# Both halves of k's remainder over 128 rows, and weight remainders computed ahead into DRAM, in a two-block network on one core

## The chip, the cores and the metric

One core of a Trainium2 chip runs the whole kernel. The metric is the device time of one execution in microseconds. The engines that matter here are TensorE (PE in the profile, with its weight loads as PEld), VectorE (DVE), ScalarE (ACT), and SyncE (SP), whose queue issues the DMAs.

## The reference, cut

Two blocks follow each other on a sequence of 512 positions of width 1024. The first has two layers, each a mixer (mLSTM, HGRN2 and sliding-window attention side by side), an MLP and a gated per-layer embedding. The second has two layers, each an attention (dilated in layer 0, differential in layer 1), a cross attention to 256 memory positions and a SwiGLU network. All is float32.

```python
for l in range(DEPTH):                                   # first block
    y = _rms_norm(x, in_norm_g[l]) @ w_in[l] + b_in[l]
    ...
    x = x + jnp.concatenate([m_out, h_out, s_out], axis=-1) @ w_out[l]
    u = _rms_norm(x, mlp_norm_g[l]) @ w_up[l]
    x = x + jnp.square(jax.nn.relu(u)) @ w_down[l]
    ...
# second block, differential attention (layer 1); layer 0 takes the same scores with dilated masks
sc = jnp.einsum('bhcqd,bhckd->bhcqk', qblk, k, preferred_element_type=f32) * scale
p = jax.nn.softmax(sc, axis=-1)
a = p[:, :, 0] - lam * p[:, :, 1]
return jnp.einsum('bhqk,bhkd->bhqd', a.astype(v.dtype), v, preferred_element_type=f32)
```

Heads are 64 wide, so two heads share 128 partitions.

## The kernel before

**Number format.** A float32 operand is held as two fp32r tiles: a rounded high part (made by a ScalarE cast) and the remainder, called the lower half (made by a VectorE subtraction). A product is three matmuls, hi·hi, lo·hi and hi·lo (`mm3`). For the scores of 64-wide heads there are stacks instead: `q_stacks` puts the high part of q in the head's own 64 rows of one tile `qs` and the lower half in the other 64; `k_stacks` puts the high part of k into both halves of `kh`. One 128-row matmul of `qs` and `kh` then gives q_hi·k_hi + q_lo·k_hi. The lower half `kl` is only in the head's own 64 rows, and a second matmul over these 64 rows adds q_hi·k_lo. That is so in the attentions (`score`, lines 1735 to 1742) and in the mLSTM (lines 1381 to 1383). The sliding-window heads ask for `both=True` and fill `kl` in both halves by a second VectorE subtraction.

**Stages.** One program runs the stages b10, mlp0, ple0, b11, mlp1, ple1, attn0, cross0, ffn0, attn1, cross1, ffn1 in this order; b10 and b11 are the mixers of the first block, the last digit is the layer. In mlp a block of 8 GEMMs with `w_up` and 8 with `w_down` is repeated four times; a GEMM is one weight tile of 128x1024 and 24 matmuls of 512 columns. In attn each of 8 pairs of heads makes q and k by two GEMMs, rotates them, builds the stacks, computes the scores, the softmax and the product with v, while GEMMs of the pairs after it stand between. In cross the memory's K and V are made from `xk` and `xv` in pieces of 512 columns (`mem_kv`), as a filling between other work.

**Weights.** `Weights.load` calls `wload` (line 789): SP loads the raw weight into `wr`, ScalarE casts it to `wh`, VectorE subtracts to `wl`. Tile counts are fixed by line 673, `NT, NWH, NWR, NKR, NKH = 58, 5, 3, 2, 2`: five of `wh` and of `wl`, three raw ones; the small pieces of `xk` and `xv` have two raw tiles `kr` and two each of `kh` and `kl` of their own. In a mixer 34 + 12 + 32 loads over the two layers carry its weights; all of them need the subtraction.

**What sets the order.** Code is not issued as written. A `Recorder` notes every operation; a list scheduler (`schedule`) with planned costs, dependences and tile counts puts them in order on each engine, and `emit` writes that order out. So every instruction has the line of the one `getattr` call in `emit` (L670 before, L674 after), and the profile is read by the tiles' names: `wr`, `wh`, `wl` for weights, `kr`, `kh`, `kl` for small pieces and for k, `g` and `s` for PSUM banks, `hi`, `lo` for activations. A DMA stands in SP's order and waits there until its tile is free; nothing behind it is issued meanwhile.

## Time and profile before

| | |
|---|---|
| median of 3 runs | 3096.06 us (3095.2 to 3097.9) |
| profiled execution | 3094.59 us, its span 3092.8 us |
| granted TensorE clock, mean | 0.981 |
| TensorE busy | 3024.8 us (98%), 16672 matmuls |
| weight loads of TensorE busy | 2463.1 us (80%) |
| VectorE busy | 1922.2 us (62%), 3811 instructions |
| ScalarE busy | 1490.9 us (48%), 2731 instructions |
| DMA | 269.96 MB, mean 87 GB/s |

Busy shares are means over stages that differ much, so the trace is read by stage. The stages end at about 300, 632, 690, 1000, 1330, 1390, 1660, 1855, 2250, 2515, 2697 and 3093 us of the span; neighbours overlap by some us. Matmuls are pipelined: a row's duration is longer than the distance to the next start, and it is the distance that tells what a matmul costs.

### The profile page before, as it was taken

To read this page: it belongs to the slowest core of one execution; us is meant where nothing else is said; L and a number is where in the kernel's file an instruction comes from. 1 tells how busy PE (TensorE), PEld (TensorE's weight loads), DVE (VectorE), ACT (ScalarE), POOL (GpSimd) and SP (SyncE) were. 2 spreads that over 40 slices of the span, in tenths; PEclk is the share of its full clock that TensorE was granted. 3 is DMA by queue.
4 is the path that set the end of the run, shared out by engine and by line. 5 is a ranking of instruction groups with operands and counts; after the bars stand their busy time and mean duration, and the time that the engine had idled before them with its cause. 6 is when DMAs were issued, how large, how long until landed. Compare 5 with 4: busy or idle time off the path is not lost.

```text
span 3092.8 us, 42875 instructions
## 1 busy us (share of the span) xinstructions
PE 3024.8 (98%) x16672; PEld 2463.1 (80%) x16672; DVE 1922.2 (62%) x3811; ACT 1490.9 (48%) x2731; POOL 75.0 (2%) x91
## 2 busy tenths in 40 slices
PE   8999999999999999999999999999999999999998
PEld 6767888887767888887776888888887778988887
DVE  7868444478878544467657756333489867653435
ACT  7557333346567333345667544222366665542223
POOL 0010000000010000000000000000000000000000
PEclk9989999999989999999999999999999999999999
DMA  3302222321312323222111423222322223332223
GB/s 119 96 12 80 102 95 96 99 91 59 106 46 63 112 96 99 98 94 77 42 55 63 125 74 102 100 97 96 102 87 71 66 65 103 97 116 96 96 98 100
DMA packets 86611, 269.96 MB, mean 87 GB/s; under 512 B 9608, under 2 KB 12680, under 8 KB 86408
## 3 DMA queue, kind: packets, MB, share of 16 engines
q1 hardware_dynamic: 86408, 267.22, 26.7%
q8 instruction: 131, 2.15, 0.3%
q14 instruction: 72, 0.59, 0.1%
HBM read 265.09 MB, written 2.10 MB: 86 GB/s over the span
## 4 chain that ended last, share of the span: by engine, by line
PE 90%; DVE 6%; ACT 2%; DMA 1%; issue 1%; POOL 0%; POOLq 0%; DVEq 0%; ACTq 0%; SPq 0%
PE s L670 47%; PE g L670 39%; PE t L670 4%; DVE wl L670 1%; DVE y L670 1%; DVE G L670 0%; ACT kh L670 0%; DVE X L670 0%; ACT wh L670 0%; DMA kr<-in_xk_dram 0%; DVE kl L670 0%; DVE B L670 0%; DMA wr<-in_w_in_tm_dram 0%; DVE x L670 0%; ACT L670 0%
## 5 line engine op out<-in xcount | busy, mean ns | idle before, releaser
L670 ACT CAST wh<-wr 128x1024 fp32r<-128x1024 f32 (+2 forms) x482 | 483.5, 1006 | 1086.0 <-PE s L670 394.3
L670 DVE TENSOR_TENSOR wl<-wr,wh 128x1024 fp32r<-128x1024 f32 (+2 forms) x482 | 560.3, 1164 | 233.8 <-ACT wh L670 226.0
L670 PE MATMUL g<-hi,wh 128*128 128x512 f32 (+1 forms) x1756 | 679.0, 387 | 12.3 <-ACT hi L670 9.3
L670 PE MATMUL g<-hi,wl 128*128 128x512 f32 (+1 forms) x1756 | 678.0, 386 | 1.5 <-DVE wl L670 1.5
L670 PE MATMUL g<-lo,wh 128*128 128x512 f32 (+1 forms) x1756 | 678.6, 387 | 0.1
L670 PE MATMUL s<-hi,wh 128*128 128x512 f32 (+1 forms) x1732 | 652.2, 377 | 2.5 <-ACT hi L670 2.4
L670 PE MATMUL s<-lo,wh 128*128 128x512 f32 (+1 forms) x1732 | 651.5, 377 | 2.0 <-DVE lo L670 2.0
L670 PE MATMUL s<-hi,wl 128*128 128x512 f32 (+1 forms) x1732 | 652.2, 377 | 0.0
L670 PEld LDWEIGHTS g<-hi,wh 128*128 128x128 f32 x1756 | 333.5, 190 | 78.9 <-ACT hi L670 10.9
L670 PEld LDWEIGHTS g<-hi,wl 128*128 128x128 f32 x1756 | 333.9, 190 | 65.4 <-issue 6.4
L670 PEld LDWEIGHTS g<-lo,wh 128*128 128x128 f32 x1756 | 333.5, 190 | 63.4 <-issue 4.9
L670 PEld LDWEIGHTS s<-hi,wh 128*128 128x128 f32 x1732 | 326.1, 188 | 62.1 <-ACT hi L670 4.1
L670 PEld LDWEIGHTS s<-lo,wh 128*128 128x128 f32 x1732 | 326.2, 188 | 60.6 <-DVE lo L670 3.1
L670 PEld LDWEIGHTS s<-hi,wl 128*128 128x128 f32 x1732 | 326.2, 188 | 57.6 <-issue 1.2
L670 ACT ACTIVATE P<-P,s 128x512 f32<-128x512 f32 (+1 forms) x224 | 137.6, 627 | 25.0 <-DVE s L670 24.4
L670 POOL TENSOR_TENSOR s<-s,mhalf 128x4 f32<-128x4 f32 (+2 forms) x53 | 69.0, 1303 | 2864.9 <-DVE s L670 2423.9
L670 ACT ACTIVATE hi<-x,cols 128x512 fp32r<-128x512 f32 (+1 forms) x112 | 73.5, 659 | 68.5 <-DVE x L670 67.8
L670 PE MATMUL t<-const,P 128*128 128x128 f32 x560 | 96.8, 281 | 1.5 <-ACT P L670 1.0
L670 PE MATMUL g<-wh,hi 128*128 128x256 f32 (+1 forms) x304 | 91.2, 301 | 0.1
L670 PE MATMUL g<-wh,lo 128*128 128x256 f32 (+1 forms) x304 | 91.1, 300 | 0.0
L670 PE MATMUL g<-wl,hi 128*128 128x256 f32 (+1 forms) x304 | 90.9, 299 | 0.0
L670 DVE TENSOR_TENSOR u<-s,R 128x512 f32<-128x512 f32 x39 | 27.0, 692 | 101.0 <-PE s L670 101.0
(300 smaller groups left out, 4058.2 us busy)
## 6 DMA issues: line engine op xcount, KB each, us to landing
wr<-in_w_down_dram SPq DMA_DIRECT2D x96, 512.0 KB, 3.3
wr<-in_gu_dram SPq DMA_DIRECT2D x88, 512.0 KB, 3.3
wr<-in_w_up_dram SPq DMA_DIRECT2D x64, 512.0 KB, 3.3
wr<-in_w_in_fm_dram SPq DMA_DIRECT2D x34, 512.0 KB, 3.3
wr<-in_qk_dram SPq DMA_DIRECT2D x32, 512.0 KB, 3.3
wr<-in_xo_dram SPq DMA_DIRECT2D x24, 512.0 KB, 3.5
wr<-in_w_down_dram SPq DMA_DIRECT2D x32, 384.0 KB, 3.2
wr<-in_w_out_dram SPq DMA_DIRECT2D x32, 256.0 KB, 2.7
```

Source lines behind the costliest of these rows:

```text
L670: getattr(getattr(nc, o.eng), o.fn)(*[res(a) for a in o.args], **{k: res(v) for k, v in o.kw.items()})
```

## The change

Three things are altered. First, `k_stacks` fills `kl` in both halves for all its callers, by a ScalarE copy of the own half; the second matmul of a score then runs over 128 rows, in the attentions and in the mLSTM, and adds q_lo·k_lo as well. Second, `lows` makes the lower halves of later weights in pieces of 512 columns (a load into `kr`, a cast to `kh`, a subtraction to `kl`, a store to a DRAM tile `dl`), 206 pieces in all: 62 in mlp0 (for the weights of b11), 64 in mlp1 (`xk`, `xv`, `ao`, `xq` of layer 0) and 80 in ffn0 (`qk`, `v`, `xk`, `xv` of layer 1). `work` puts them behind the evacuations of the GEMMs, one to three at a time. Third, `wload` of such a weight loads `wl` (or `kl`) from that DRAM tile in SP's queue in place of the subtraction. The rest (`psum`, `after`) keeps the recorder right with the new DRAM pool.

```diff
+        self.psum = space is not None and space is not DRAM
...
+        if self.after is not None:
+            deps.add(self.after)
...
-        return self.b.wload(src, n, self.small), k1 - k0, c1 - c0
+        lows = self.b.pre.get(id(self.ap))
+        return self.b.wload(src, n, self.small, lows and lows[self.i - 1]), k1 - k0, c1 - c0
...
+        self.dp = nc.pool("dp", 1, DRAM)
+        self.pre, self.jobs = {}, []
...
-    def wload(self, src, n, small=False):
+    def wload(self, src, n, small=False, low=None):
         nc = self.nc
         if small:
             raw = self.kr.tile([P, T], F32, name=self.nm("kr"), tag="kr")[:, :n]
...
             lo = self.wp.tile([P, 1024], F32R, name=self.nm("wl"), tag="wl")[:, :n]
         nc.sync.dma_start(raw, src)
         nc.scalar.copy(hi, raw)
-        nc.vector.tensor_tensor(lo, raw, hi.bitcast(F32), op=ALU.subtract)
+        if low is None:
+            nc.vector.tensor_tensor(lo, raw, hi.bitcast(F32), op=ALU.subtract)
+        else:
+            nc.sync.dma_start(lo.bitcast(F32), low)
         return hi, lo
+
+    def lows(self, name, plan):
+
+        nc, ap = self.nc, self.a[name]
+        out = self.pre[id(ap)] = []
+        o = 0
+        for k0, k1, c0, c1 in plan:
+            n = (k1 - k0) * (c1 - c0)
+            out.append(self.dp.tile([P, n], F32, name=self.nm("dl"), tag=f"{name}_{len(out)}"))
+            for s in range(0, n, T):
+                m = min(T, n - s)
+                raw = self.kr.tile([P, T], F32, name=self.nm("kr"), tag="kr")[:, :m]
+                hi = self.kp.tile([P, T], F32R, name=self.nm("kh"), tag="kh")[:, :m]
+                lo = self.kp.tile([P, T], F32R, name=self.nm("kl"), tag="kl")[:, :m]
+                nc.after = nc.ops[-1]
+                nc.sync.dma_start(raw, bass.AP(tensor=ap.tensor, offset=ap.offset + o + s, ap=[[n, P], [1, m]]))
+                nc.after = None
+                nc.scalar.copy(hi, raw)
+                nc.vector.tensor_tensor(lo, raw, hi.bitcast(F32), op=ALU.subtract)
+                nc.sync.dma_start(out[-1][:, s:s + m], lo.bitcast(F32))
+                yield
+            o += n * P
+
+    def ahead(self, *names):
+
+        for name, plan in names:
+            self.jobs.append(self.lows(name, PLANS[plan]))
+
+    def work(self, n=1):
+        while n and self.jobs:
+            try:
+                next(self.jobs[0])
+                n -= 1
+            except StopIteration:
+                self.jobs.pop(0)
+
+    def work_all(self):
+        while self.jobs:
+            self.work()
...
-    def k_stacks(self, k, both=False):
-
+    def k_stacks(self, k):
         nc = self.nc
         out = []
         for h in range(2):
...
             nc.scalar.copy(hi[own], k[own])
             nc.scalar.copy(hi[oth], k[own])
             nc.vector.tensor_tensor(lo[own], k[own], hi[own].bitcast(F32), op=ALU.subtract)
-            if both:
-                nc.vector.tensor_tensor(lo[oth], k[own], hi[own].bitcast(F32), op=ALU.subtract)
+            nc.scalar.copy(lo[oth], lo[own].bitcast(F32))
             out.append((hi, lo))
...
                 nc.tensor.matmul(sb, kh[:, s], qs[hh][:, t0:], start=True, stop=False)
-                own = slice(64 * hh, 64 * hh + 64)
-                nc.tensor.matmul(sb, kl[own, s], qs[hh][own, t0:], start=False, stop=True)
+                nc.tensor.matmul(sb, kl[:, s], qs[hh][:, t0:], start=False, stop=True)
                 nc.vector.tensor_tensor(W[j], sb[:, j * P - t0:], W[j], op=ALU.mult)
                 As[hh, j] = W[j]
         o = self.obank()
...
         wd = Weights(self, self.a[f"w_down{l}"], PLANS["w_down"])
         st2 = self.stats()
+        if l == 0:
+            self.ahead(("w_in_fm1", "w_in_fm"), ("w_in_tm1", "w_in_tm"), ("w_out1", "w_out"))
+        else:
+            self.ahead(("xk0", "xk"), ("xv0", "xv"), ("ao0", "sq"), ("xq0", "sq"))
         for c in range(4):
             hid = []
 
...
                 nc.vector.tensor_scalar(u, o, 0.0, None, op0=ALU.max)
                 nc.scalar.activation(u, u, AF.Square)
                 hid.append(self.split(u))
+                self.work()
 
             self.gemm(wu, ops, 8, evac)
 
...
                 nc.vector.tensor_tensor(self.x[j], self.x[j], u, op=ALU.add)
                 if c == 3:
                     self.updated(st2, j)
+                else:
+                    self.work(1 + j % 2)
 
             self.gemm(wd, hid, KT, evac2)
+        self.work_all()
         return st2
 
     def ple(self, l, st):
...
-    def score(self, h, q, k, c, mask):
+    def score(self, q, k, c, mask):
         nc = self.nc
         s = self.sbank()
         kh, kl = k
         nc.tensor.matmul(s, q[:, c * P:c * P + P], kh, start=True, stop=False)
-        own = slice(64 * h, 64 * h + 64)
-        nc.tensor.matmul(s, q[own, c * P:c * P + P], kl[own], start=False, stop=True)
+        nc.tensor.matmul(s, q[:, c * P:c * P + P], kl, start=False, stop=True)
         p = self.f("P")
         mx, dn = self.small(1), self.small(1)
         if mask is None:
...
         ys = [None] * KT
+        if l == 0:
+            self.ahead(("qk1", "qk"), ("v1", "v"), ("xk1", "xk"), ("xv1", "xv"))
         for c, nh in enumerate((8, 8, 6)):
             hid = []
             for j in range(nh):
...
                 nc.scalar.activation(t, t, AF.Silu, bias=0.0)
                 nc.vector.tensor_tensor(t, u, t, op=ALU.mult)
                 hid.append(self.split(t))
+                self.work(3)
 
             def evac(j, o):
                 if c == 0:
...
 
             if c < 2:
                 self.gemm(wd, hid, KT, evac)
+        self.work_all()
         st2 = {"halves": [], "ops": []}
         mark = wd.i, wd.o
         for u, h in enumerate(HALVES):
```

What the change does to the order on the engines is shown at three places, each before and after, word for word.

SP's queue in mlp1, at the turn from `w_up` to `w_down`; each row is one DMA, the tile it writes and what it reads. Before:

```order
L670 DMA wr_9911<-in_w_up_dram 128x1024
L670 DMA wr_9945<-in_w_up_dram 128x1024
L670 DMA wr_9979<-in_w_up_dram 128x1024
L670 DMA wr_10013<-in_w_up_dram 128x1024
L670 DMA wr_10049<-in_w_down_dram 128x1024
L670 DMA wr_10087<-in_w_down_dram 128x1024
L670 DMA wr_10125<-in_w_down_dram 128x1024
```

After:

```order
L674 DMA dl_11297<-kl_11290 128x512
L674 DMA kr_11303<-in_xv_dram 128x512
L674 DMA wr_11328<-in_w_down_dram 128x1024
L674 DMA dl_11342<-kl_11336 128x512
L674 DMA kr_11364<-in_xv_dram 128x512
L674 DMA wr_11374<-in_w_down_dram 128x1024
L674 DMA dl_11400<-kl_11390 128x512
L674 DMA kr_11407<-in_xv_dram 128x512
L674 DMA wr_11420<-in_w_down_dram 128x1024
L674 DMA dl_11439<-kl_11434 128x512
```

Between two weight loads there now stand a store of one piece's lower half and the load of a later piece.

VectorE in attn1, about the middle of the stage, between the rotation and the stacks of one pair of heads and the transposed probabilities (`Tl`) of another. Before:

```order
L670 TENSOR_TENSOR qs_21807<-z_21669,qs_21807 64x512
L670 TENSOR_TENSOR wl_21876<-wr_21448,wh_21638 128x1024
L670 TENSOR_TENSOR Tl_21849<-t_21860,Th_21834 128x2x128
L670 TENSOR_TENSOR Tl_21854<-t_21860,Th_21839 128x2x128
L670 TENSOR_TENSOR kl_21903<-z_21773,kh_21870 64x512
L670 TENSOR_TENSOR kl_21910<-z_21773,kh_21890 64x512
L670 SCALAR_TENSOR_TENSOR vl_21917<-s_21736,s_20045,vh_21816 128x256
L670 SCALAR_TENSOR_TENSOR vl_21917<-g_21795,s_20045,vh_21816 128x256
```

After:

```order
L674 SCALAR_TENSOR_TENSOR vl_23223<-g_23096,s_21317,vh_23121 128x256
L674 TENSOR_SCALAR s_23244<-s_23244 128x1
L674 TENSOR_TENSOR kl_23261<-kr_23212,kh_23249 128x512
L674 RECIPROCAL s_23257<-s_23257 128x1
L674 TENSOR_TENSOR kl_23276<-z_23089,kh_23216 64x512
L674 TENSOR_TENSOR Tl_23237<-t_23247,Th_23228 128x2x128
L674 TENSOR_TENSOR Tl_23241<-t_23247,Th_23233 128x2x128
```

The subtraction for a weight of this stage (`wl`) is gone; in its place stands one for a piece (`kl` from `kr`, 128x512) that ffn0's part of the program had begun to list.

TensorE in cross0, in the products that make the memory's K (`kh`, `kl` are a piece of `xk`, `hi` and `lo` the memory's activations, 128x256). Before, at the seam of two pieces:

```order
L670 MATMUL g_15245<-hi_8198,kh_15285 128x256
L670 MATMUL g_15245<-hi_8198,kl_15294 128x256
L670 MATMUL g_15245<-lo_9027,kh_15285 128x256
L670 MATMUL g_15245<-hi_8114,kh_15292 128x256
L670 MATMUL g_15245<-hi_8114,kl_15301 128x256
L670 MATMUL g_15245<-lo_8122,kh_15292 128x256
L670 MATMUL g_15245<-hi_8114,kh_15292 128x256
```

After, at the seam of two pieces:

```order
L674 MATMUL g_16265<-hi_8617,kl_16328 128x256
L674 MATMUL g_16265<-lo_8629,kh_16331 128x256
L674 MATMUL s_16387<-hi_8471,kh_16365 128x256
L674 MATMUL g_16326<-lo_16359,wh_16034 128x512
L674 MATMUL g_16392<-hi_16300,wh_16061 128x512
L674 MATMUL g_16392<-hi_16300,wl_16045 128x512
L674 MATMUL g_16326<-hi_16384,wh_16034 128x512
L674 MATMUL s_16387<-hi_8471,kl_16362 128x256
L674 MATMUL s_16387<-lo_8485,kh_16365 128x256
L674 MATMUL s_16387<-hi_8471,kh_16365 128x256
```

GEMM matmuls of 512 columns now stand between the pieces, which followed each other directly.

## Rows read from the trace of the kernel before

**Rows 1.** The chain that ended last, its shares by engine.

```profile
PE 90%; DVE 6%; ACT 2%; DMA 1%; issue 1%; POOL 0%; POOLq 0%; DVEq 0%; ACTq 0%; SPq 0%
```

**Rows 2.** Windows of eight stages: b10, mlp0, b11, attn0, cross0, ffn0, attn1, cross1.

```profile
core 0: us, PE busy (x) PEld busy (x) DVE busy (x) ACT busy (x) POOL busy (x), PEclk, DMA share, GB/s
0.00:300.00 300.00, 273.04 (x1839) 206.09 (x1840) 230.05 (x630) 192.12 (x445) 21.95 (x44) 0.91 0.24 74
300.00:632.00 332.00, 332.00 (x1481) 274.81 (x1480) 164.27 (x199) 111.62 (x142) 1.01 (x1) 1.00 0.30 100
690.00:1000.00 310.00, 290.82 (x1844) 221.37 (x1843) 253.86 (x661) 203.34 (x463) 16.92 (x14) 0.92 0.22 66
1390.00:1660.00 270.00, 269.98 (x1467) 198.06 (x1466) 184.99 (x444) 173.00 (x322) 1.01 (x1) 1.00 0.19 63
1660.00:1855.00 195.00, 192.08 (x1188) 161.92 (x1189) 124.68 (x264) 109.00 (x210) 3.51 (x3) 0.99 0.28 87
1855.00:2250.00 395.00, 394.31 (x1937) 331.26 (x1936) 174.58 (x222) 129.49 (x180) 4.29 (x4) 1.00 0.31 100
2250.00:2515.00 265.00, 262.92 (x1609) 210.15 (x1608) 236.87 (x586) 177.00 (x373) 11.50 (x10) 1.00 0.20 65
2515.00:2697.00 182.00, 177.27 (x1216) 159.16 (x1215) 118.91 (x230) 94.47 (x183) 4.25 (x4) 0.99 0.32 101
```

**Rows 3.** Timeline of TensorE in attn0: start, duration (us), operation, shapes.

```profile
1509.60 0.39 PE L670 MATMUL g<-lo,wh 128*128 128x512 f32 x1
1509.83 0.40 PE L670 MATMUL g<-hi,wh 128*128 128x512 f32 x1
...
1510.52 0.40 PE L670 MATMUL s<-kh,qs 128*128 128x512 f32 x1
1510.85 0.50 PE L670 MATMUL s<-kl,qs 64*128 64x512 f32 x1
1511.28 0.50 PE L670 MATMUL g<-hi,wh 128*128 128x512 f32 x1
1511.62 0.40 PE L670 MATMUL s<-kh,qs 128*128 128x512 f32 x1
```

**Rows 4.** Timeline of TensorE in b10's sliding-window heads.

```profile
260.62 0.28 PE L670 MATMUL s<-kh,qs 128*128 128x256 f32 x1
260.74 0.28 PE L670 MATMUL s<-kl,qs 128*128 128x256 f32 x1
```

**Rows 5.** Tile kl, its score matmuls: count, ns min/median/max, starts, forms.

```profile
L670 PE MATMUL s<-kl,qs x192: 277/492/562, 233.2 to 2511.4; 64*128 64x512 f32 x128, 128*128 128x256 f32 x64
L670 PE MATMUL s<-qs,kl x32: 335/579/792, 157.7 to 894.5; 64*128 64x256 f32 x16, 64*128 64x512 f32 x8, 64*128 64x384 f32 x8
```

**Rows 6.** Groups by form: shapes, count, busy us, mean ns, idle before.

```profile
L670 DVE TENSOR_TENSOR wl<-wr,wh 128x1024 fp32r<-128x1024 f32 x406 | 495.3, 1222 | 219.4 <-ACT wh L670 212.3 <-PE s L670 6.2
L670 ACT CAST kh<-z 64x512 fp32r<-64x512 f32 x72 | 44.5, 618 | 24.3 <-DVE z L670 23.0
L670 DVE TENSOR_TENSOR kl<-kr,kh 128x512 fp32r<-128x512 f32 x64 | 43.4, 687 | 16.3 <-ACT kh L670 15.1 <-PE s L670 0.9
L670 ACT CAST kh<-kr 128x512 fp32r<-128x512 f32 x64 | 39.1, 617 | 27.6 <-DMA kr<-in_xv_dram 10.8 <-DMA kr<-in_xk_dram 10.0 <-PE g L670 2.7
```

**Rows 7.** Timeline of TensorE in b11's mLSTM.

```profile
893.49 0.58 PE L670 MATMUL s<-qs,kl 64*128 64x256 f32 x1
893.99 0.58 PE L670 MATMUL s<-qs,kh 128*128 128x256 f32 x1
```

**Rows 8.** Window of b11, VectorE's instructions on tile wl alone.

```profile
690.00:1000.00 310.00, 37.87 (x40) 0.92 0.22 66
```

**Rows 9.** Loads of xk's pieces, from issue to landing.

```profile
DMA to landing us min/median/max: 2.5/3.1/5.2
```

**Rows 10.** DMA issues of xq: count, KB each, median us to landing.

```profile
wr<-in_xq_dram SPq DMA_DIRECT2D x16, 512.0 KB, 3.9
```

**Rows 11.** Waits of SP's queue: total us, times, longest.

```profile
SPq L670 <- DVE wl L670: 2381.5, 436, 51.7
```

More of the change, by code (lines that the diff above doesn't have):

```diff
@@ L17 @@
 PSUM = bass.MemoryType.PSUM
+DRAM = bass.MemoryType.DRAM
 P = 128
@@ L307, in __init__ @@
         self.ops, self.pools = [], []
-        self.single = None
+        self.single = self.after = None
         for e in ("tensor", "vector", "scalar", "gpsimd", "sync", "either"):
@@ L333, in add @@
             for wb, w in v.tile.writes:
-                if v.tile.pool.space is not None and w.eng == "tensor" or \
+                if v.tile.pool.psum and w.eng == "tensor" or \
                         wb[0] <= b[1] and b[0] <= wb[1] and wb[2] <= b[3] and b[2] <= wb[3]:
@@ L341, in add @@
                     if (wb[0] <= b[1] and b[0] <= wb[1] and wb[2] <= b[3] and b[2] <= wb[3]) or \
-                            (v.tile.pool.space is not None and eng == "tensor"):
+                            (v.tile.pool.psum and eng == "tensor"):
                         deps.add(w)
@@ L364, in add @@
                 t.left += 1
-        o.banks = [t for t in o.tiles if t.pool.space is not None] if eng != "tensor" else []
+        o.banks = [t for t in o.tiles if t.pool.psum] if eng != "tensor" else []
+        if self.after is not None:
+            deps.add(self.after)
         o.deps = [d for d in deps if d is not o]
@@ L398, in locks @@
             return False
-        psum = lambda v: v.tile.pool.space is not None
+        psum = lambda v: v.tile.pool.psum
         ptr = o.fn in ("tensor_scalar", "scalar_tensor_tensor")
@@ L410, in cost @@
         n = int(np.prod(o.args[0].shape[1:])) if isinstance(o.args[0], View) else 512
-        psum = any(v.tile.pool.space is not None for v in ins + outs)
+        psum = any(v.tile.pool.psum for v in ins + outs)
         if o.eng == "tensor":
@@ L429, in cost @@
             acc = 93.0 if "accum_out" in o.kw else 0.0
-            return (51.0 if (ins or outs)[0].tile.pool.space is not None else 93.0) + n * ACT_EL + PTR_A * ptr + acc, 130.0
+            return (51.0 if (ins or outs)[0].tile.pool.psum else 93.0) + n * ACT_EL + PTR_A * ptr + acc, 130.0
         if o.eng == "vector":
@@ L1098, in block1 @@
         sw = self.swa_prep(l, lambda: fm_id(F_SK), "swk")
-        ks = self.k_stacks(sw, True)
+        ks = self.k_stacks(sw)
         m0 = self.mlstm(l, 0, mq[0], mk[0], tm, rows)
@@ L1661, in attn @@
                 for c2 in range(2):
-                    pr = [[self.score(h, qs[h], ks[h], 2 * c2 + c, dil[2 * c2 + c]) for h in range(2)] for c in range(2)]
+                    pr = [[self.score(qs[h], ks[h], 2 * c2 + c, dil[2 * c2 + c]) for h in range(2)] for c in range(2)]
                     for c in range(2):
@@ L1694, in attn @@
                         c = 2 * c2 + cc
-                        p0, d0 = self.score(0, qs[0], ks[0], c, None)
-                        p1, d1 = self.score(1, qs[1], ks[1], c, None)
+                        p0, d0 = self.score(qs[0], ks[0], c, None)
+                        p1, d1 = self.score(qs[1], ks[1], c, None)
                         nc.vector.reciprocal(d0, d0)
```

## The prediction

> **What bounds the kernel now.** I read the chain of waits first: TensorE carries 90% of the chain that ended last [rows 1]. Then the table by stage [rows 2]: in two of the large GEMM stages, mlp0 and ffn0, TensorE is busy 332.0 of 332.0 us and 394.3 of 395.0; in the two attention stages 270.0 of 270.0 and 262.9 of 265.0. VectorE is far behind everywhere but in attn1 (236.9 of 265.0) and in the mixer block b11 (253.9 of 310.0, where TensorE idles 19.2 us). So what counts is TensorE's own time, and VectorE's load only in b11 and attn1.
>
> A busy TensorE isn't one at its peak, so I then read starts in the timeline. In attn0 a 128x512 GEMM matmul follows the one before it after 0.23 us (1509.60 to 1509.83). Around the product with k's lower half, which has 64 rows (64*128), it does not: from kh at 1510.52 to the next kh at 1511.62, three matmuls of 512 columns take 1.10 us, where 3 x 0.23 = 0.69 would do: 0.41 us more for one 64-row matmul, spread over its neighbours [rows 3]. The control is in the same kernel: the sliding-window heads already hold both halves of k, their lower product has 128 rows, and the next matmul starts 0.12 us behind, as it should with 256 columns [rows 4]. There are 128 such matmuls of 64 rows in the attention stages (192 less the 64 of the sliding window) and 32 in the mLSTM [rows 5].
>
> A rule speaks against this reading. The Trainium skill (TensorE: Matmul & The Clock Gate, What overlaps and what doesn't) says that a weight load overlaps with running matmuls only if its row group differs, and another table of that page that a single product with few rows takes the same time as one with 128; by the two nothing would be won, and D below is that case. The trace disagrees with the first: 128-row products one behind the other keep 0.23 and 0.12 us. The Trainium skill (TensorEngine Tiling (Array Packing), Key Properties) also says that a change of tiling mode drains the engine; the trace agrees, if 64 rows are such a mode: 0.41 us for going there and back.
>
> **The change part by part.**
>
> *k over 128 rows in attention.* Columns stay, so TensorE loses only the 0.41 us: 64 x 0.41 = 26 us in attn0 and as much in attn1. Added: one ScalarE copy for each half head, 16 x 0.618 = 9.9 us per stage [rows 6], which stands between VectorE's subtraction and the lower product. In attn0 TensorE then needs 270 - 26 = 244 us; ScalarE 173 + 10 = 183 and VectorE's 185 stay under it. TensorE has GEMMs of the next heads to fill in. I take 24 of 26; the floor is 10, should the copy hold up each of the 16 chains by about a microsecond.
>
> *attn1.* Its 24 weights of qk and v lose their subtraction, 24 x 1.222 = 29.3 us of VectorE [rows 6]. But the change's order shows that not all jobs fit in ffn0: behind ffn0's last weight load 35 of its 80 stores are still to come, and subtractions of theirs stand in attn1's VectorE order between those of the heads. At most that gives back 35 x 0.687 = 24.0 us, and on ScalarE 35 x 0.617 = 21.6 beside 9.9 for copies. So VectorE goes from 236.9 to about 232, ScalarE from 177 to 208, TensorE from 265 to 239. VectorE rises from 89% to 97% of the stage's length: it is nearly a second bound, and a cast that waits for its load stands in ScalarE's queue ahead of the heads' exponentials. I take 15 of 26; ends 3 and 26.
>
> *mLSTM.* 16 matmuls of 64 rows in each of b10 and b11. They start 0.50 us apart with 256 columns, against 0.12 [rows 4, 7]; part of that is the lower clock there (granted 0.91 and 0.92 on average). Price each between 0.41 us and 2 x 0.38 = 0.76: 6.6 to 12.2 us per layer. TensorE idles 27.0 and 19.2 us in these stages for other engines, so some of it turns into waiting: I take 4 in each, ends 0 and 12.
>
> *Weights of b11.* 40 subtractions leave VectorE, 37.9 us of 253.9 [rows 2, 8]. That can free no more than TensorE's idle 19.2 us. Few of the 40 lie where TensorE idles, so I take 5 us; ends 0 and 19.
>
> *Lower halves loaded, cross0 and cross1.* The 64 pieces of xk and xv use two small buffers. Before, a free one was refilled by a cast and a subtraction (0.617 + 0.687 us); now the lower half comes by a load, 3.1 us after its issue in the median, 2.5 at best [rows 9], and it can't be issued until TensorE has read the buffer. A piece is 12 matmuls x 0.12 = 1.44 us; the order lets 3 to 5 GEMM matmuls (0.23 each, some 0.9) stand between pieces, so a refill has 1.44 + 2 x 0.9 = 3.2 us. Load and need are even; 0.1 us lost at each piece makes 64 x 0.1 = 6 us. Lower end: 7.6 us won (TensorE's idle time there, 2.9 and 4.7 us). Upper end: 64 x 0.7 = 45 lost, if these loads rise to the 3.9 us of xq's [rows 10]. I stay near even, since 3.1 is the row of these very pieces. VectorE's relief (32 x 0.687 = 22 us in cross1) buys little: it is busy 118.9 of 182 there.
>
> *The jobs in mlp0, mlp1 and ffn0.* 206 pieces: load, cast 0.617, subtraction 0.687, store, 256 KB each way. VectorE goes from 164 to 164 + 62 x 0.687 = 207 of 332 us in mlp0, ScalarE to 150. No wait ends late there; the data rate rises from 100 GB/s by 62 x 0.52 MB / 332 us = 97, the DMA share from 0.30 to about 0.6. What hides this is the lead of the weight loads: SP waits 2381.5 us in total for VectorE's subtractions to free a raw buffer, so loads are nearly always early [rows 11]. One new wait sits in SP's queue: the order there is weight, store, small load, and the store waits for the cast and subtraction of the load before it, with the next weight load behind it. One turn costs 3.1 + 0.62 + 0.69 = 4.4 us and the hand-overs between engines, and TensorE eats a weight in 24 x 0.23 = 5.5. It fits, by 1.1 us for the hand-overs. I take 0; its other end is the slower rival below.
>
> Sum: -24 -15 -4 -4 -5 +6 = -46. The profiled execution took 3094.6 us (span 3092.8), so 3048.6; the median of the runs lies 1.5 above it, so 3050.
>
> **The rivals.**
> (B) attn1 becomes VectorE's and the pieces wait for their loads: attn1 gives 5 instead of 15, the crosses cost 20 instead of 6: 3050 + 24 = 3074. For it: 97% in attn1, the two buffers. Against it: VectorE at 89% of attn1 now leaves TensorE only 2.1 us idle.
> (C) The relief is worth nearly all it can be: 25 + 23 in attention, 19 + 4 in b11, 4 in b10, and the crosses win 4: 3096 - 79 = 3017. Against it: the leftover jobs in attn1.
> (D) The 0.41 us doesn't come from the rows but from the change of operands, which stays. Then only b11's 5 us are won and the crosses' 6 lost: 3097, within 0.2%. Against it: [rows 4], where the operands change as often.
> (E) Slower: SP's queue paces TensorE in mlp0 and mlp1, where there is about one job for one weight (62 + 52 turns). It decides from a turn of 5.5 us. If the small loads land after 5.2 us, the longest of xk's [rows 9], since two more streams share the DMA engines, a turn is 6.5: 114 x 1.0 = 114 us, less a lead of three weights in each stage (2 x 16.5), so 81 on 3050: 3131. For it: the doubled DMA share. Against it: 5.2 is one row's end, the median 3.1, and many of these loads ran beside weight loads too.
>
> **How the numbers follow.** Forecast as summed, 3050: 0.66. B 0.14, C 0.10, D 0.04, E 0.06. What a measurement of this kernel can tell from no change is about 0.2%, here 6 us: 3090 to 3102. Faster: the forecast, B and C, 0.90; same: D, 0.04; slower: E, 0.06. The forecast's own ends come from attn1 (3 to 26), attn0 (10 to 26), b11 and the crosses: some 3030 to 3070. The range reaches to B and close to C: 3020 to 3080.
>
> **What would show it.** In the profile after, the groups of 64 rows are gone, the product with kl starts 0.23 us behind kh's, and attn0 is near 246 us. attn1 near 250 with VectorE over 90%: right; over 260: B. mlp0, mlp1 and ffn0 keep their lengths within 2 us, else E, and TensorE then waits for the cast or the subtraction of a weight. In cross0 and cross1 I look for TensorE waiting for loads of kl. I'm wrong at the root if the pitch around kl stays 0.4 us at 128 rows.

## The result, and the profile after

The changed kernel takes 3045.36 us in the median of 4 runs (3044.07 to 3050.5), against 3096.66 before: ratio 0.984, 95% interval 0.982 to 0.986. 51 us went; 46 were forecast. The unchanged kernel was run beside each batch of kernels below; its median there lies between 3094.97 and 3097.4.

The table by stage of the kernel after (columns as in [rows 2]; b10, mlp0, b11, attn0, cross0, ffn0, attn1, cross1). In every kernel below a stage ends where TensorE starts the GEMM matmul with the same number, counting those that read a weight, as at the stage's end in the kernel before.

```profile
core 0: us, PE busy (x) PEld busy (x) DVE busy (x) ACT busy (x) POOL busy (x), PEclk, DMA share, GB/s
0.00:296.90 296.90, 267.61 (x1839) 206.41 (x1840) 228.52 (x628) 194.76 (x451) 21.94 (x44) 0.92 0.23 75
296.90:628.90 332.00, 332.00 (x1481) 274.80 (x1480) 200.08 (x259) 148.59 (x203) 1.01 (x1) 1.00 0.60 195
686.90:967.10 280.20, 271.30 (x1839) 211.11 (x1838) 220.24 (x623) 202.41 (x467) 19.76 (x14) 0.98 0.40 128
1356.90:1610.80 253.90, 252.62 (x1475) 199.35 (x1474) 185.04 (x457) 183.51 (x345) 1.01 (x1) 1.00 0.25 84
1610.80:1802.90 192.10, 187.20 (x1184) 159.38 (x1183) 90.05 (x209) 106.67 (x208) 2.71 (x3) 1.00 0.48 157
1802.90:2201.20 398.30, 392.30 (x1888) 326.97 (x1888) 194.12 (x255) 152.89 (x215) 4.32 (x4) 0.99 0.47 157
2201.20:2462.10 260.90, 250.38 (x1628) 213.65 (x1627) 233.09 (x601) 206.21 (x429) 9.46 (x10) 1.00 0.56 186
2462.10:2646.20 184.10, 180.58 (x1245) 161.33 (x1244) 107.34 (x208) 98.22 (x188) 3.72 (x4) 1.00 0.47 150
```

Against [rows 2]: mlp0 is 332.0 us as before, with the DMA share at 0.60 instead of 0.30 and TensorE never idle. b11 fell from 310 to 280 us: TensorE's idle time from 19.2 to 8.9, and its mean granted clock rose from 0.92 to 0.98. attn0 fell from 270 to 254, attn1 only from 265 to 261, with TensorE's idle time up from 2.1 to 10.5 us; ffn0 grew by 3.

The products with k's lower half, in attn0 after (start, duration, operation):

```profile
1474.78 0.40 PE L674 MATMUL s<-kh,qs 128*128 128x512 f32 x1
1475.02 0.39 PE L674 MATMUL s<-kl,qs 128*128 128x512 f32 x1
1475.24 0.40 PE L674 MATMUL g<-hi,wh 128*128 128x512 f32 x1
```

kl starts 0.24 us behind kh and the GEMM 0.22 us behind kl; in [rows 3] these were 0.33 and 0.43.

Stage lengths against the kernel before, in us, of all kernels run (each from its profiled execution; mlp0 and ple0 stay within 0.1, and mlp1, ple1 and ffn1 within 1.0 but for ple1 in pieces64, +2.9; attn and cross are taken together, since work moves over their border). One execution scatters: in b10 the order of TensorE's matmuls is the same in after, k_only and all kernels from b11_qkv1 to b11, and their b10 lies anywhere from -1.3 to -4.4. So a difference below some 3 us between two rows of this table is not told apart from none.

| kernel | median, us | ratio, interval | b10 | b11 | attn0 + cross0 | ffn0 | attn1 + cross1 |
|---|---|---|---|---|---|---|---|
| after | 3045.36 | 0.984 (0.982 to 0.986) | -3.2 | -29.8 | -18.9 | +3.3 | -2.0 |
| k_only | 3042.79 | 0.983 (0.981 to 0.984) | -2.5 | -11.9 | -20.2 | 0.0 | -16.3 |
| lows_only | 3100.66 | 1.0015 (1.0005 to 1.0026) | +3.5 | -23.8 | +1.8 | +2.0 | +20.6 |
| k_attn | 3053.83 | 0.987 (0.985 to 0.989) | -3.7 | +3.0 | -22.4 | 0.0 | -17.4 |
| b11_qkv1 | 3026.3 | 0.977 (0.976 to 0.978) | -3.3 | -29.5 | -19.3 | +2.6 | -18.5 |
| m0m1_qkv1 | 3025.47 | 0.977 (0.976 to 0.979) | -2.2 | -29.3 | -18.3 | +1.5 | -18.3 |
| pieces64 | 3043.22 | 0.983 (0.982 to 0.985) | -2.8 | -30.2 | -20.3 | +2.9 | -4.9 |
| dma_only | 3038.07 | 0.981 (0.980 to 0.983) | -2.7 | -30.2 | -18.5 | +2.6 | -7.8 |
| early32 | 3026.66 | 0.978 (0.976 to 0.979) | -1.3 | -30.3 | -20.7 | +1.6 | -17.5 |
| b11 | 3026.1 | 0.977 (0.976 to 0.979) | -4.4 | -28.0 | -17.9 | +0.2 | -17.2 |
| swa64 | 3125.88 | 1.0095 (1.008 to 1.011) | +18.6 | +12.2 | +0.5 | -0.1 | +1.5 |

### The profile page after: what moved, and what is told of

Its sections match the earlier page's. It is cut to its first block, busy times and chain, and to the rows that moved or that the text cites. A ratio compares the mean times of both kernels' runs of the same rounds, so it can differ in the third digit from the quotient of the medians.

```text
span 3042.3 us, 44343 instructions
## 1 busy us (share of the span) xinstructions
PE 2966.3 (98%) x16672; PEld 2453.6 (81%) x16672; DVE 1923.8 (63%) x3870; ACT 1627.0 (53%) x2975; POOL 73.3 (2%) x91
## 4 chain that ended last, share of the span: by engine, by line
PE 84%; ACT 6%; DVE 6%; DMA 3%; issue 1%; POOL 0%; SPq 0%; POOLq 0%; ACTq 0%; DVEq 0%
PE s L674 42%; PE g L674 38%; PE t L674 4%; ACT kh L674 1%; ACT P L674 1%; DMA kl<-dl 1%; ACT wh L674 1%; DVE wl L674 1%; DVE sh L674 1%; DVE s L674 1%; DVE y L674 0%; DVE z L674 0%; DVE cv L674 0%; ACT kl L674 0%; DMA kr<-in_xq_dram 0%
## 5 line engine op out<-in xcount | busy, mean ns | idle before, releaser
L674 DVE TENSOR_TENSOR wl<-wr,wh 128x1024 fp32r<-128x1024 f32 (+2 forms) x403 | 474.7, 1179 | 405.3 <-PE s L674 131.8
L674 ACT CAST kh<-kr 128x512 fp32r<-128x512 f32 (+2 forms) x270 | 166.0, 616 | 125.9 <-DMA kr<-in_xk_dram 24.9
L674 DVE TENSOR_TENSOR kl<-kr,kh 128x512 fp32r<-128x512 f32 (+2 forms) x206 | 141.1, 685 | 66.8 <-ACT kh L674 65.1
L674 DVE SCALAR_TENSOR_TENSOR lo<-x,cols,hi 128x512 fp32r<-128x512 f32 (+1 forms) x112 | 74.7, 672 | 24.7 <-ACT hi L674 24.2
```

Source lines behind the costliest of these rows:

```text
L674: getattr(getattr(nc, o.eng), o.fn)(*[res(a) for a in o.args], **{k: res(v) for k, v in o.kw.items()})
```

## The experiments

### The two parts apart: k_only and lows_only

k_only keeps the change of `k_stacks`, `score` and the mLSTM and lists no work ahead:

```diff
         if l == 0:
-            self.ahead(("w_in_fm1", "w_in_fm"), ("w_in_tm1", "w_in_tm"), ("w_out1", "w_out"))
+            pass
         else:
-            self.ahead(("xk0", "xk"), ("xv0", "xv"), ("ao0", "sq"), ("xq0", "sq"))
+            pass
...
-            self.ahead(("qk1", "qk"), ("v1", "v"), ("xk1", "xk"), ("xv1", "xv"))
+            pass
```

> Only k over 128 rows; no lower half is made ahead, every weight keeps its subtraction. Theory 1 (two separate gains: k's rows give the attention stages and b10 theirs, the weights' relief gives b11 most of its 30 us): b10 -3, attn0 with cross0 -19, attn1 -14 since no leftover pieces stand in it, b11 -5 to -10, the others within 1: 3096 - 44 = 3052, between 3048 and 3060. Theory 2 (b11's 30 us come from k's rows in the mLSTM, which end its stretches at half the clock): b11 -25 here, so 3096 - 61 = 3035. Theory 3 (attn1 is bound by VectorE, with or without leftovers): attn1 -4 as in the changed kernel.

lows_only puts the three functions back as they were and keeps everything else:

```diff
-            nc.scalar.copy(lo[oth], lo[own].bitcast(F32))
+            if both:
+                nc.vector.tensor_tensor(lo[oth], k[own], hi[own].bitcast(F32), op=ALU.subtract)
...
-        nc.tensor.matmul(s, q[:, c * P:c * P + P], kl, start=False, stop=True)
+        own = slice(64 * h, 64 * h + 64)
+        nc.tensor.matmul(s, q[own, c * P:c * P + P], kl[own], start=False, stop=True)
```

> Only the lower halves made ahead and loaded; k's remainder stays over 64 rows in attention and mLSTM, as before the change. Theory 1: b11 -20 to -25, attn0 0, attn1 +3 to +8 (leftover pieces, no shorter products), ffn0 +3, cross within 3: 3096 - 15 = 3081, between 3074 and 3088. Theory 2: b11 -5, and the rest as in theory 1: 3098. Theory 1 also asks that the half-speed stretches of b11 go from 47.7 us to about 15 or less here; theory 2 that they stay above 35.

k's rows alone make the whole gain: 3042.79 us, which can't be told from the full change (the intervals overlap). The work ahead alone is 0.15% slower than before. So k's rows make the size of the full change's 51 us; the work ahead wins in b11 and loses as much in other places. Windows of k_only (b11, attn0, attn1; columns as above):

```profile
687.60:985.60 298.00, 278.79 (x1838) 217.77 (x1838) 252.70 (x661) 205.29 (x471) 17.23 (x14) 0.94 0.22 71
1375.40:1626.50 251.10, 250.65 (x1459) 198.49 (x1459) 180.70 (x442) 175.98 (x331) 1.01 (x1) 1.00 0.21 68
2215.10:2466.30 251.20, 244.87 (x1609) 211.29 (x1608) 236.10 (x592) 186.24 (x392) 11.65 (x10) 1.00 0.22 70
```

and of lows_only (b11, attn1):

```profile
693.60:979.70 286.10, 277.58 (x1839) 212.92 (x1837) 221.85 (x625) 198.74 (x461) 19.90 (x14) 0.97 0.39 125
2233.30:2514.20 280.90, 274.23 (x1625) 215.31 (x1624) 234.89 (x601) 197.65 (x414) 9.91 (x10) 0.98 0.51 170
```

In b11 VectorE is busy 252.7 us with k's rows alone and 221.9 with the work ahead alone; the stage shrinks by 11.9 and 23.8 us, by 29.8 with both. So theory 2 falls: b11 gets the larger part from the weights' relief, 29.8 - 11.9 = 18 us beside k's rows, and with the work ahead alone its mean clock is 0.97. The time that b11 spends at half the clock, on which the expectation also turned, goes from 47.7 us to 17 in lows_only and to 34 in k_only. In attn1 lows_only has 281 us where the kernel before had 265. Theory 1 holds in its split, but both its times were missed. Its 3052 for k_only was 9 us too much, outside the 3048 to 3060 that I had put (every stage but b10 gave a little more). And it was too mild on what the work ahead costs in attn1: I had put +3 to +8 and, for the whole kernel, 3081; it was +20.6 with cross1, and 3100.66. Theory 3 falls with k_only's -16.3: attn1 isn't bound by VectorE, which is busy 236.1 of 251.2 us there.

### Whether rows make the 0.4 us: swa64

The kernel before, with its control turned round:

```diff
-                nc.tensor.matmul(s[:, hs], qq, kl[:, kb:kb + 256], start=False, stop=True)
+                own = slice(0, 64)
+                nc.tensor.matmul(s[:, hs], qs[h][own, c * P:c * P + P], kl[own, kb:kb + 256], start=False, stop=True)
```

> The kernel before, with one thing turned the other way: the sliding-window heads' lower product, 128 rows in the control of the prediction, runs over rows 0 to 63 only (columns and count stay; for the second head of each pair this multiplies q's lower half with k's, so that a term of the scores is left out). If the number of rows makes the 0.3 to 0.4 us: the starts behind these 64 matmuls go from 0.12 us to 0.25 or more, TensorE has 64 x 0.25 to 64 x 0.41 = 16 to 26 us more work in b10 and b11, part of it in their idle time: slower by 6 to 24 us, 3102 to 3120. If it is the change of operands: starts stay at 0.12 and the time within 3 us of 3096.

Timeline of TensorE in b10's sliding-window heads of swa64, at the full clock:

```profile
275.81 0.38 PE L670 MATMUL s<-kl,qs 64*128 64x256 f32 x1
276.12 0.38 PE L670 MATMUL s<-kh,qs 128*128 128x256 f32 x1
276.44 0.38 PE L670 MATMUL s<-kl,qs 64*128 64x256 f32 x1
```

The starts are now 0.31 us apart where [rows 4] has 0.12: 0.19 us at each of the two changes, 0.38 for the pair, with 256 columns, beside the 0.41 of [rows 3] with 512. So it is the rows, and the price hardly goes with the columns. The kernel got 30 us slower (3125.88 against 3096.02), more than the 24 us at most that I had put (64 x 0.38 = 24.3): in b10, +18.6 us for 32 products, the mean granted clock also fell from 0.91 [rows 2] to 0.89:

```profile
0.00:318.70 318.70, 293.25 (x1840) 214.35 (x1841) 231.32 (x630) 193.11 (x446) 21.99 (x44) 0.89 0.22 69
```

A row of the kernel before shows what the price is paid for, the turn and not the product. In attn1 two kh, two kl and two kh follow each other (x2 are two matmuls in one line):

```profile
2354.72 0.73 PE L670 MATMUL s<-kh,qs 128*128 128x512 f32 x2
2355.38 0.73 PE L670 MATMUL s<-kl,qs 64*128 64x512 f32 x2
2356.03 0.73 PE L670 MATMUL s<-kh,qs 128*128 128x512 f32 x2
```

From the first kh to the third there are four matmuls in 1.31 us, where 4 x 0.23 = 0.92 would do: 0.39 us for two products with 64 rows, as for one. The two other places in attn1 with such a pair among matmuls of 512 columns have 0.40 and 0.38; the 41 places of the kernel before with a single one have 0.41 in the median (0.39 to 0.52). The Trainium skill (TensorEngine Tiling (Array Packing), Key Properties) puts a drain of the engine on a change of tiling mode; these runs agree with it.

### The mLSTM's share: k_attn

k_only, with the mLSTM's line put back:

```diff
-                nc.tensor.matmul(sb, kl[:, s], qs[hh][:, t0:], start=False, stop=True)
+                own = slice(64 * hh, 64 * hh + 64)
+                nc.tensor.matmul(sb, kl[own, s], qs[hh][own, t0:], start=False, stop=True)
```

> As k_only, but the mLSTM's lower product runs over 64 rows again (the copy into the other half stays). If the mLSTM's 16 products of each layer made the 12 us that k_only won in b11 and the 2.4 in b10: b10 and b11 as before the change, attn0, cross0, attn1 as in k_only: 3042.8 + 14 = 3057, between 3053 and 3061. If the sliding-window stacks did it (their second subtraction went from VectorE to ScalarE): b11 stays at -8 to -12, 3043 to 3048.

b11 is at +3.0 us instead of -11.9, so the mLSTM's 16 products are worth 14.9 us in b11, more than the 12 that I had put. That b10 would be as before failed: it stays at -3.7, so the 16 are worth nothing that shows in its length, and its few us come from elsewhere, perhaps from the sliding-window stacks, whose second subtraction k_attn too leaves to ScalarE. TensorE's idle time in b10 is 26.6 us in k_attn and 28.9 in k_only, so some of the saving turned into waiting there. The window of b11 in k_attn, to be read against k_only's:

```profile
686.50:999.50 313.00, 288.77 (x1844) 220.42 (x1843) 252.85 (x659) 206.75 (x470) 19.27 (x14) 0.93 0.21 66
```

Of the 15 us TensorE's busy time has 10 (288.8 to 278.8) and its idle time 5 (24.2 to 19.2); a part of the busy time is the clock, granted 0.93 here and 0.94 in k_only. Against the kernel before b11 wins 11.9 in k_only; the 3.0 by which k_attn lies above it are within the scatter.

### Where the relief of attn1 went: b11_qkv1, m0m1_qkv1, pieces64, dma_only, early32, b11

These six differ only in which lower halves are made ahead, and where. Their edits, in the three lists (mlp0, mlp1, ffn0):

```diff
 # b11_qkv1: mlp0 as in the change, mlp1 none
-            self.ahead(("qk1", "qk"), ("v1", "v"), ("xk1", "xk"), ("xv1", "xv"))
+            self.ahead(("qk1", "qk"), ("v1", "v"))
 # m0m1_qkv1: mlp0 and mlp1 as in the change
-            self.ahead(("qk1", "qk"), ("v1", "v"), ("xk1", "xk"), ("xv1", "xv"))
+            self.ahead(("qk1", "qk"), ("v1", "v"))
 # pieces64: mlp0 and mlp1 as in the change
-            self.ahead(("qk1", "qk"), ("v1", "v"), ("xk1", "xk"), ("xv1", "xv"))
+            self.ahead(("qk1", "qk"), ("v1", "v"), ("xk1", "xk"))
 # early32: mlp0 as in the change
-            self.ahead(("xk0", "xk"), ("xv0", "xv"), ("ao0", "sq"), ("xq0", "sq"))
+            self.ahead(("xk1", "xk"), ("xv1", "xv"))
...
-            self.ahead(("qk1", "qk"), ("v1", "v"), ("xk1", "xk"), ("xv1", "xv"))
+            self.ahead(("qk1", "qk"), ("v1", "v"))
 # b11: mlp0 as in the change, mlp1 and ffn0 none
```

and in dma_only, in `lows`:

```diff
+                if name in ("xk1", "xv1"):
+                    nc.sync.dma_start(out[-1][:, s:s + m], raw)
+                    yield
+                    continue
                 nc.scalar.copy(hi, raw)
                 nc.vector.tensor_tensor(lo, raw, hi.bitcast(F32), op=ALU.subtract)
                 nc.sync.dma_start(out[-1][:, s:s + m], lo.bitcast(F32))
```

> The whole change, but lower halves are made ahead only for the weights of b11 (62 pieces in mlp0) and for qk and v of attn1 (48 pieces in ffn0, all stored before its last weight load); nothing in mlp1, and xk, xv, ao, xq keep their subtractions. If the leftover pieces in attn1 are what took its gain (theory A): attn1 -16 to -20 against before instead of -4, cross1 0 instead of +2, b11 -30: 3045 - 15 = 3030, between 3026 and 3036. If attn1 is bound by VectorE or by the heads' chains anyway (theory B): attn1 -4 to -8, total 3042 to 3047.

3026.3 us, 0.6% below the full change: attn1 with cross1 is at -18.5 instead of -2.0. Theory A.

> The whole change without the 32 pieces of xk1 and xv1 in ffn0: 174 pieces, 3 of them left for attn1 instead of 35. What is tested: that the pieces left over in attn1 cost it about 15 us. Theory A (leftovers): attn1 -18 against before as in b11_qkv1 instead of -4, cross1 0, the rest as in the changed kernel: 3045 - 16 = 3029, between 3025 and 3034; against b11_qkv1 (3026.3) the pieces of mlp1 then cost 0 to 5 us, in attn0. Theory B (the pieces of mlp1, not those of ffn0, made the difference between b11_qkv1 and the changed kernel): 3040 to 3045.

3025.47: putting mlp1's 64 pieces back changes nothing, taking ffn0's 32 of xk1 and xv1 out changes 16 us. Theory A again, and mlp1's pieces are worth nothing either way (attn0 with cross0 -18.3 against -19.3).

> The whole change without the 16 pieces of xv1: 64 pieces in ffn0, of which 19 are left for attn1: 14 between its first and its eighth load of v, as in the changed kernel, and 5 behind the eighth instead of 21. If each leftover piece costs alike: attn1 -4 - 16 x 0.43 = -11, 3038. If those between the heads cost (14 in both): attn1 -4 to -7, 3041 to 3045. If it is the crowd at the end: attn1 -15 or more, 3034 or less.

With xk1's 16 pieces and without xv1's, attn1 with cross1 is at -4.9: against m0m1_qkv1 (-18.3) the first 16 cost 13 us, the next 16 cost 3. By the border of the two stages attn1 alone reads as -15.8, as in my third answer, and cross1 as +10.9; the windows of the two:

```profile
2202.00:2451.80 249.80, 243.56 (x1600) 209.20 (x1599) 217.91 (x560) 190.75 (x394) 9.47 (x10) 1.00 0.50 167
2451.80:2644.10 192.30, 185.26 (x1274) 166.89 (x1273) 123.42 (x250) 105.32 (x206) 4.16 (x4) 0.99 0.36 114
```

So none of my three answers fits as it stands: it is neither each piece alike nor the crowd at the end of attn1, and the loss sits across the border.

> The whole change, but the 32 pieces of xk1 and xv1 are only loaded and stored again: their cast and subtraction are left out (so the lower halves of these two weights are wrong). 35 stores still stand behind ffn0's last weight load, with as many DMAs in SP's queue in attn1; ScalarE and VectorE lose 32 x 1.30 us of work. If the leftovers cost through the two engines' queues (a cast that waits for its load ahead of the heads' work): attn1 -14 to -19 instead of -4, 3030 to 3036. If they cost through SP's queue and the DMA: attn1 stays within 3 us of -4, 3042 to 3048.

-7.8: without the cast and subtraction of 32 pieces (and without the small tiles kh and kl that these take) 6 of the 16 us come back. 10 stay, and they need neither engine's time. That fell between my two answers: attn1 alone is at -16.1, as in the first, but cross1 at +8.3, which neither had. Left were the load of kl in cross1, and pieces that are still being moved while attn1 and cross1 run. What TensorE waits for over the two stages (in us in total, times, longest) begins so:

```profile
PE s L674 <- DMA kl<-dl: 4.8, 5, 1.4
PE g L674 <- DMA kl<-dl: 1.3, 1, 1.3
```

6.1 of its 11.3 idle us there are waits for a lower half's load.

> The 32 pieces of xk1 and xv1 are made in mlp1 (in place of xk0, xv0, ao0, xq0, which keep their subtractions), qk and v of attn1 in ffn0, b11's in mlp0: cross1 loads its lower halves as in the changed kernel, but they lie in DRAM some 900 us before, and only 3 pieces are left over for attn1. Measured so far, attn1 and cross1 together against before: changed kernel -2.0, without xv1's pieces -5.0, with the 32 only moved by DMA -7.9, without the 32 -18.4. If it is lateness (the leftovers and what waits for them, the memory's products among it) that costs the 16 us: -15 to -20 here, ffn0 within 1 of before, 3023 to 3029. If it is the loading of kl in cross1, which needs a DMA for each of two buffers: -6 to -10, 3034 to 3040.

-17.5: with the lower halves long in DRAM, loading them costs nothing in cross1. What costs is that they are still being made. In early32 TensorE waits 1.1 us for loads of kl in these stages, in dma_only 6.1; so half of the 10 us that stay in dma_only are lower halves that come late. Some 3 more are work that stands in ffn0 in early32 (the seam, below). Why they come late, by their own stores or by SP's queue standing still for others, no run separates; in dma_only SP waits 44.5 us in these stages for pieces' loads that it is to store again, in the full change 26.5 for their subtractions, so that the 10 us need not be those of the full change. Windows of attn1 and cross1 in early32:

```profile
2198.80:2449.00 250.20, 247.66 (x1631) 213.49 (x1630) 216.76 (x576) 192.21 (x403) 9.84 (x10) 1.00 0.39 131
2449.00:2628.20 179.20, 176.55 (x1218) 157.77 (x1217) 104.13 (x201) 94.51 (x180) 3.72 (x4) 1.00 0.43 141
```

TensorE's idle time is 2.5 us in attn1 and 2.7 in cross1, against 10.5 and 3.5 in the full change. There only 1.0 us of it are waits for a load of kl; TensorE waits mostly for what ScalarE and VectorE make for the heads. ScalarE itself stood 9.9 us of attn1 in the full change with the cast of a leftover piece at the head of its queue, whose load had not landed:

```profile
ACT kh L674 <- DMA kr<-in_xv_dram: 4.9, 4, 2.5
ACT kh L674 <- DMA kr<-in_xk_dram: 3.2, 2, 2.5
ACT kh L674 <- DMA kr<-in_v_dram: 1.8, 1, 1.8
```

So in the full change TensorE waits mostly for the heads' chain, in dma_only mostly for lower halves of the memory's weights.

> k over 128 rows and lower halves made ahead for b11's weights alone (62 pieces in mlp0). From the stages of k_only and b11_qkv1, if they add: b11 -30, attn0 with cross0 -20, attn1 with cross1 -16, ffn0 0, b10 -3: 3096 - 69 = 3027, between 3023 and 3031; the 48 pieces of qk and v of attn1 are then worth 2 us in attn1 and cost as much in ffn0. If they are worth what they take off VectorE in attn1 (36 us of 236): 3033 or more here.

3026.1 us with 62 pieces only, at par with the best. The 48 pieces of qk and v take VectorE in attn1 from 236.1 us (k_only's window) to 216.8 (early32's, which has them too) and win 1.3 us there (-18.5 against -17.2), which is less than the scatter; in ffn0 they cost 2.4.

One thing that waits can be seen directly. At the seam from cross0 to ffn0, while the column sums, the root and the scaling of the activations follow each other, the kernel before fed TensorE with the memory's products of the next layer. After, these need lower halves that ffn0 has yet to make. Two windows at that seam, before and after:

```profile
1886.00:1894.00 8.00, 8.00 (x102) 7.84 (x100) 4.61 (x8) 4.07 (x7) 1.70 (x2) 1.00 0.34 111
```

```profile
1834.00:1842.00 8.00, 3.72 (x49) 2.78 (x46) 3.11 (x6) 2.13 (x4) 1.70 (x2) 0.67 0.20 68
```

and TensorE's timeline there after (what it waited for is in brackets):

```profile
1835.38 0.43 PE L674 MATMUL t<-const,s 128*128 128x128 f32 x2 [0.80 <-POOL s L674]
1836.27 1.59 PE L674 MATMUL t<-const,acc 128*64 128x1 f32 x32 [0.46 <-ACT R L674]
1839.29 1.11 PE L674 MATMUL t<-const,s 128*128 128x128 f32 x4 [1.42 <-POOL s L674]
1843.25 0.80 PE L674 MATMUL s<-hi,wh 128*128 128x512 f32 x1 [2.85 <-ACT hi L674]
```

Before, TensorE is busy 8.0 of 8.0 us there at the full clock. After, it is busy 3.7, waits for POOL and ScalarE, and its granted clock in the window is 0.67. The four waits in the timeline make 5.5 of the 6.0 us that TensorE idles in ffn0, and half the clock costs some more. Against that ffn0 has lost the memory's products, 48 matmuls with some 6 us of work (at 0.12 each [rows 4]), which now stand in attn1 and cross1; what is left of the sum is its +3.3. Of the products with the memory's kl, 16 stand at this seam in k_only and b11 (ffn0 0.0 and +0.2), 8 in b11_qkv1, m0m1_qkv1 and early32 (+2.6, +1.5, +1.6; there the pieces of qk and v share the small buffers), none where ffn0 makes xk1's (+2.0 to +3.3). So ffn0, attn1 and cross1 are best read together: -16.3 in k_only, -16.8 in m0m1_qkv1, -15.9 in early32, -5.2 in dma_only and +1.3 in the full change.

## Why the prediction held, point by point

**The bound.** That TensorE's time counts and a 64-row product costs 0.4 us held: k's rows alone give 53 us, from 3096.02 to 3042.79. I had 24 + 15 + 4 + 4 = 47 for them. That the work ahead is worth nothing on the whole held too, as a total: the prediction's -5 + 6 = +1 stands against +2.6 (full change less k_only) within the intervals. The total is right by a balance, though, and four of its terms were mis-sized.

**attn0, forecast -24.** With cross0 -18.9, in k_only -20.2 and in k_attn -22.4. The price per product is as read [rows 3]; of 64 x 0.41 = 26 us 73 to 86% arrived in these three. Products that stand side by side and share a turn are a small part of it: in the timeline of the kernel before 10 of the 128 go so, but 8 of them in attn1. The rest I can't place; TensorE's idle time in attn0 is 1.3 us.

**attn1, forecast -15 with the crosses +6.** k's rows alone give -16.3 there, so the gain was to be had; but the change gives -2.0, since the leftover pieces take 16 (in part work that came over from ffn0). I saw them in the order and costed them as engine time, 24.0 us of VectorE and 21.6 of ScalarE. The step that failed is this one: without that engine time only 6 of the 16 us come back (dma_only), and all of it only when the pieces are done before these stages (early32). The wait that I had named, a cast in ScalarE's queue ahead of the heads' exponentials, is in the trace with 9.9 us, and my sum had no price of its own for it, nor for lower halves that come late. And VectorE's relief, put against it at 29.3 us, was worth at most 1.3 (b11 against b11_qkv1), because VectorE at 236 of 251 us sets nothing in attn1. This is half of rival B: its pieces do wait for their loads, and attn1 alone gives 4.6, near B's 5; but VectorE isn't the bound (busy 233.1 of 260.9), and the crosses lose 0.9 instead of 20.

**The crosses' loads, forecast +6, ends -7.6 to +45.** Nothing, where the lower half is ready: m0m1_qkv1 in cross0 and early32 in cross1 load kl for xk and xv without a loss that shows. The pieces' loads took 3.3 us from issue to landing against 3.1 in [rows 9], and the GEMM matmuls between the pieces covered it. Where it isn't ready, in dma_only, TensorE waits 6.1 us for it.

**mLSTM, forecast -4 in each layer.** -14.9 in b11 and none that shows in b10. I took it that some of the saving would turn into waiting. In b10 none of it is left, and that b10's -3.2 lies near the forecast's -4 is luck: with these products over 64 rows (k_attn) it has -3.7. In b11 nothing did: the idle time is 19.2 us with k's rows alone as before, and the time at the lower clock shrank from 47.7 to 34.

**b11's weights, forecast -5, ends 0 to 19.** -18 beside k's rows, -23.8 alone. I had capped it at TensorE's idle time, 19.2 us, and taken a quarter, since few subtractions lie where TensorE idles. The step left the clock out. A window of the kernel before, in b11's mLSTM,

```profile
884.00:898.00 14.00, 13.74 (x43) 7.04 (x44) 10.93 (x25) 8.81 (x21) 1.63 (x1) 0.50 0.01 2
```

and the row of TensorE's timeline just ahead of it:

```profile
883.71 1.02 PE L670 MATMUL t<-const,sq 128*64 128x2 f32 x16 [1.88 <-ACT s L670]
```

TensorE runs there at the lower of its two levels, 1.2 GHz, right behind a wait for ScalarE, and needs 14 us for what would take some 7 at 2.4. b11's mean of 0.92 over 310 us means 310 x 0.08 = 25 us lost; after it is 280 x 0.02 = 6. The trace has TensorE busy at the lower level for 43.7 us of b11 before and 10.2 after, and half of that difference is 17. So of the 30 us some 17 are clock, 10 idle time and 3 matmul work that is gone. I had the 0.92 in a row. That the waits bring the clock down is read from where they stand and not tested by itself: three of b11's six stretches at the lower level begin in or right behind a wait of 1.9 to 4.0 us, while k's rows alone shortened these stretches with the idle time as it was.

**mlp0, mlp1, forecast 0, and rival E.** 0.0 and -0.6 us, TensorE waits for nothing in either. The small loads of mlp0 landed after 3.6 us, not 3.1; the rows below are of the whole kernel after, and `w_in_fm`'s are all in mlp0:

```profile
kr<-in_w_in_fm_dram SPq DMA_DIRECT2D x34, 256.0 KB, 3.6
kr<-in_xk_dram SPq DMA_DIRECT2D x64, 256.0 KB, 3.2
kl<-dl SPq DMA_DIRECT2D x64, 256.0 KB, 3.3
```

A turn is then 3.6 + 0.62 + 0.69 = 4.9 us and the hand-overs, still under 5.5. ffn0's +3.3 I had at 0; it is the seam, not the queue.

**Rivals.** D falls with swa64. Of the two rules that the prediction weighed for it, the first (the Trainium skill, TensorE: Matmul & The Clock Gate, What overlaps and what doesn't) has a weight load overlap with running matmuls only if its row group differs; from the two I took that the rows would change nothing. In swa64 the rows alone were changed, and the starts went from 0.12 to 0.31 us apart. E falls with mlp0. C's full relief in attention didn't come, its b11 did, and more (30 us instead of 23). The forecast was 5 us off, -46 against -51, by terms that cancelled: b11 gave 21 us more than its two terms (-29.8 against -9), attn1 with cross1 gave 10 less (-2.0 against -15 + 3), attn0 with cross0 2 less (-18.9 against -24 + 3), ffn0 cost 3, b10 gave 1 less. That the total came so near is luck.

The two parts don't need each other's whole: k's rows with the 62 pieces for b11 alone (b11) take 3026.1 us, 0.6% less than the full change, 2.3% less than before.

## What to carry to other kernels

A matmul over part of the rows between full ones costs two turns of TensorE, here 0.4 us with 256 columns as with 512; filling the other rows by a copy on an engine with time to spare buys that back. Work made ahead pays where its consumer waits, here in b11 alone, and turns into a loss where it isn't done in time: whatever used to fill a gap with that data must wait too. A stage with idle time and a mean clock below 1 can win more than its idle time: b11 won 30 us with 10 us less of it.

## What the runs showed of the hardware

Going from 128 rows to 64 and back costs TensorE 0.38 us with 256 columns (swa64) and 0.41 with 512 (median of 41 places in the kernel before), and two 64-row products side by side pay for one round (0.38 to 0.41 in three places). A DMA share of 0.60 for 330 us in mlp0, twice the former one, moved the median landing of the stage's weight loads from 3.3 to 3.4 us and took nothing from TensorE's pace, 332.0 us in both.
